# Third state of the streamed weight sum: added by VectorE from a tile already loaded, in place of an accumulating transfer

## The chip, the cores and the metric

The kernel runs on one core of one Trainium2 chip. The metric is the device time of one execution in microseconds; before the change it was 1002.07 us (median of 3 runs, 1001.94 to 1007.12). The engines are TensorE (PE, with PEld for its weight loads), VectorE (DVE), ScalarE (ACT), GpSimd (POOL) and SyncE (SP, which issues most transfers). POOL issues the transfers that add to what stands in SBUF.

## The reference

One layer of a residual block on 512 positions of width 1024, in float32: a gated feed-forward block, a mixer with two kinds of attention, a second gated feed-forward block, and a gated embedding at the end.

```python
def swiglu(x, w_gate, w_up, w_down):
    return (jax.nn.silu(x @ w_gate) * (x @ w_up)) @ w_down
...
f = swiglu(rms_norm(h, g_ffn1_pre[i]), w_ffn1_gate[i], w_ffn1_up[i], w_ffn1_down[i])
h = h + 0.5 * rms_norm(f, g_ffn1_post[i])
...
h = h + rms_norm(mixed @ w_out[i], g_mix_post[i])
f = swiglu(rms_norm(h, g_ffn2_pre[i]), w_ffn2_gate[i], w_ffn2_up[i], w_ffn2_down[i])
h = h + 0.5 * rms_norm(f, g_ffn2_post[i])
e = (p[i] @ w_ple_proj[i]) * jax.nn.sigmoid(h @ w_ple_gate[i])
h = h + rms_norm(e, g_ple_post[i])
```

The two feed-forward blocks have an inner width of 2816, 22 tiles of 128.

## The kernel before, in words

**Numbers as pairs.** Each float32 operand is split into a rounded part (hi) and the rest (lo), and a product is three matmuls: hi by hi, lo by hi, hi by lo (`mm3`, lines 247 to 250). The split of a weight chunk is made by ACT (wh, line 313) and DVE (wl = source minus wh, line 314).

**Seven products for eight.** Most of the feed-forward work is done in items: two column tiles of gate and up together (nine items per block, `(p,)`), or two by two tiles of the down matrix (four items per block, `(g, q)`, called down items here). An item is a 2x2 block product that is done with seven products instead of eight. Each of the seven, called op 0 to 6, multiplies a sum of input blocks (U0 to U6, or the v tiles) by a sum of weight blocks.

**Where the weight sums come from.** The four blocks of an item's weights, (0,0), (0,1), (1,0), (1,1), are added up in SBUF while they stream in. There are three kinds of tiles: x (three buffers), y (one buffer) and r. The table `SUMS` (line 164) says for each op which tile it reads, which block starts that tile, and which block is added to it after the op's split. A tile x goes through four states: (0,0) for op 0; plus (1,0) for op 2; plus (1,1) for op 3; plus (0,1) for op 5. A tile y has two: (1,1) for op 4; plus (1,0) for op 6. Op 1 reads a plain tile r. A start is a transfer on SP's queue (line 178), an addition an accumulating transfer on POOL's queue (`sum_in`, line 223), issued when the split that read the former state is done.

**The order.** `ORDER` (line 44) sets the ops of an item as 0, 1, 2, 4, 3, 6, 5, and items are interleaved: ops 3, 6, 5 of one item alternate with ops 1, 2, 4 of the next one. A chunk of weights is one op's tile; chunks are numbered in the order of use. `get` hands a chunk out, and `ensure` keeps the splits up to three chunks ahead (`LOOK`); split code is placed behind the evacuation of the op just issued (`behind("evac")`). PE's order is as written; the other engines' orders are made by a scheduler at build time, each engine then runs its instructions in order.

**Evacuations.** The products of an item share three PSUM banks, named f_a, f_b and f_c. DVE copies or adds them out: f_g (line 584), f_y (lines 588 and 597), f_x (line 591), and for down items f_f (line 629). They stand in DVE's order between the weight splits.

The lines that the change and the steps of the prediction touch: 164 (`SUMS`), 168 to 190 (`emit_dma`), 192 to 220 (`emit_split`), 222 and 223 (`sum_in`), 313 and 314 (split), 584 to 601 and 629 (evacuations).

Of the kernel before, what the change touches and what calls it, by code (L numbers as in the profile page):

```python
# [13 lines left out]
ALU = mybir.AluOpType  # L14
# [46 lines left out]
def block_kernel(ctx, tc, xT, pT, gains, ident_d, bias_d, wgu1, wst1, wd1, wdst1, wqk, wv, wo, wgu2, wst2, wd2, wdst2, wpp, wpg, gple, out):  # L61
    nc = tc.nc
    pe, act, dve, pool = nc.tensor, nc.scalar, nc.vector, nc.gpsimd
# [40 lines left out]
    chunks = []  # L104
# [39 lines left out]
    for kind, *at in PLAN:  # L144
        if kind == "qk":
            chunks.extend(qk_chunks[2 * at[0]:2 * at[0] + 2])
        else:
# [13 lines left out]
    pos, n_dma, n_split = [0], [0], [0]  # L161


    SUMS = {0: ("x", (0, 0), (1, 0)), 1: ("r", (0, 1), None), 2: ("x", None, (1, 1)), 3: ("x", None, (0, 1)),
            4: ("y", (1, 1), (1, 0)), 5: ("x", None, None), 6: ("y", None, None)}
    running = {}

    def emit_dma(cuts=1, queues=(nc.sync,)):
# [3 lines left out]
        if isinstance(n, tuple):  # L172
            op, item, n = n
            kind, block, _ = SUMS[op]
            if block is None:
# [16 lines left out]
    def emit_split(cuts=1, between=None):  # L192
        i = n_split[0]
        src, n = chunks[i]
        n_split[0] += 1
        add = None
        if isinstance(n, tuple):
            op, item, n = n
            kind, _, add = SUMS[op]
            r = raws.pop(i) if kind == "r" else running[kind, item]  # L200
        else:
            r = raws.pop(i)
        if i in apart:
            splits[i] = apart[i]()
            for q, (hi, lo) in enumerate(zip(*splits[i])):
                split_to(hi[:], lo[:], r[:, q * T:(q + 1) * T])
            return
        if i in late:
            hi, lo = late[i]()
        else:  # L210
            hi, lo = (wp.tile([P, 1024], F32R, name=f"w{q}{i}", tag=f"w{q}", bufs=4) for q in "hl")
        for q in range(cuts):
            a, b = q * n // cuts, (q + 1) * n // cuts
            with behind("evac"):
                marks["split"] = split_to(hi[:, a:b], lo[:, a:b], r[:, a:b])
            if between is not None and q == 0:
                between()
        splits[i] = (hi, lo)
        if add is not None:
            sum_in(r[:, :n], src[add[0], add[1]])  # L220

    def sum_in(r, block):
        pool.dma_start(out=r, in_=block, accum_op=ALU.add)  # L223
# [3 lines left out]
    def ensure(i):  # L227
        i = min(i, len(chunks) - 1)
        while n_split[0] <= i:
            while n_dma[0] < min(n_split[0] + (5 if n_dma[0] in deep else RAW), len(chunks)):  # L230
                emit_dma()
            emit_split()
# [78 lines left out]
    def split_to(hi, lo, src, g=None):  # L311
        if g is None:
            a = act.copy(hi, src)  # L313
            b = dve.tensor_tensor(lo, src, hi.bitcast(F32), ALU.subtract)  # L314
        else:
            a = act.activation(hi, src, AF.Copy, scale=g)
            b = dve.scalar_tensor_tensor(lo, src, g, hi.bitcast(F32), ALU.mult, ALU.subtract)
        return a.ins, b.ins

    @contextmanager  # L320
    def behind(*names):
        with ExitStack() as stack:
            for name in names:
                for ins in marks.get(name, ()):
                    stack.enter_context(tc.issue_after(ins))
            yield
# [419 lines left out]
    for j in range(4):  # L746
        if j == 0:
            nc.sync.dma_start(out=gt[:, :56], in_=gains)
        nc.sync.dma_start(out=h[:, 2 * j, :], in_=xT[2 * j * P:(2 * j + 1) * P, :])
        if j < RAW:  # L750
            emit_dma(1 if j else 2, (nc.sync,) if j else (nc.scalar, nc.sync))
        nc.sync.dma_start(out=h[:, 2 * j + 1, :], in_=xT[(2 * j + 1) * P:(2 * j + 2) * P, :])
        if j == 0:
            act.copy(tmp("table", 0)[:, 0:1], eps[:])
            emit_split(2, first_x)
            marks["first"] = marks.pop("evac") + marks["split"]
        for k in (2 * j, 2 * j + 1):
            if k:
                split_h(u, k, 0, T, G_F1PRE)
        if j:  # L760
            ensure(j)
        else:
            nc.sync.dma_start(out=ident[:], in_=ident_d)
# [19 lines left out]
    with tc.tile_pool(name="mx", bufs=1, reuse_waits="tile") as mp:  # L783
# [258 lines left out]
        for n in range(64 + LAG_AV):  # L1042
            if n < 64:
                s, r = divmod(n, 8)
# [211 lines left out]
```

## Time and profile before

| | |
|---|---|
| median of the runs | 1002.07 us (1002.07, 1001.94, 1007.12) |
| profiled execution, its own time | 1004.57 us |
| span of its trace | 1002.9 us |
| mean granted TensorE clock | 0.997 |
| moved by DMA | 139.71 MB, mean 139 GB/s |
| read from HBM | 134.31 MB |

A row of the profile gives a line, an engine, an operation and its tiles, then the busy time, the mean time of one, and the engine's idle time before it with what ended it. The chain of waits follows the work that ended last back through what released it. The span leaves out about 1.7 us of the execution around it. By stage: the first feed-forward block lies at about 20 to 335 us, the mixer at about 335 to 600 us, the second feed-forward block at about 600 to 925 us, the rest after that. How busy the engine queues and the DMA engines are over the span, in 40 equal slices of 25 us (tenths; GB/s moved):

```profile
DMA  7338887988886313313423311168879889975202
GB/s 284 101 103 189 165 173 189 196 184 187 193 190 174 118 35 115 95 54 98 123 83 98 89 60 53 53 147 173 189 171 206 192 171 204 194 186 190 61 3 85
```

The items fill the slices with 7 to 9 tenths.

### The profile page before, as it was taken

The page shows a single profiled execution, that of the slowest core. Times are in us where ns is not written, and L with a number is a line of the kernel's source. Part 1 is how long each engine was busy: PE and PEld are TensorE (multiplying, and loading weights), DVE is VectorE, ACT ScalarE, POOL GpSimd, SP SyncE. Part 2 cuts the span into 40 slices and gives each one's busy share as a digit, 9 for nine tenths or more (in the row PEclk, how much of TensorE's full clock was granted, in tenths as well). Part 3 has the DMA queues.
Part 4 walks back from the last instruction along what each step waited for, and adds up shares of the span by engine and source line. Part 5 has one row for each costly group of instructions (what it writes and reads, how often), then busy time and mean ns, then how long its engine had stood idle before and what let it go on. Part 6 is the DMA issues. An engine that isn't in the chain of part 4 may idle for free.

```text
span 1002.9 us, 18451 instructions
## 1 busy us (share of the span) xinstructions
PE 983.8 (98%) x7242; PEld 926.2 (92%) x7242; DVE 774.9 (77%) x1355; ACT 585.6 (58%) x977; POOL 134.6 (13%) x221
## 2 busy tenths in 40 slices
PE   9999999999999999999999999999999999999996
PEld 7889999999998999888898799889999999999886
DVE  6777777677666888999999868787687777676857
ACT  6456554464456366777789755465554664455563
POOL 0001112212120003344000000011122221210000
PEclk9999999999999999999999999999999999999998
DMA  7338887988886313313423311168879889975202
GB/s 284 101 103 189 165 173 189 196 184 187 193 190 174 118 35 115 95 54 98 123 83 98 89 60 53 53 147 173 189 171 206 192 171 204 194 186 190 61 3 85
DMA packets 44855, 139.71 MB, mean 139 GB/s; under 512 B 5216, under 2 KB 5600, under 8 KB 44768
## 3 DMA queue, kind: packets, MB, share of 16 engines
q0 software_dynamic: 14976, 50.34, 30.6%
q1 hardware_dynamic: 28368, 85.83, 25.2%
q10 hardware_dynamic: 1424, 2.36, 1.0%
q8 instruction: 57, 0.93, 0.4%
q14 instruction: 30, 0.25, 0.1%
HBM read 134.31 MB, written 2.10 MB: 136 GB/s over the span
## 4 chain that ended last, share of the span: by engine, by line
PE 70%; DMA 9%; issue 9%; DVE 7%; ACT 4%; POOL 0%; SPq 0%; POOLq 0%; DVEq 0%; ACTq 0%
PE f_a L248 6%; PE f_a L249 6%; PE f_a L250 6%; DMA wy<-in_wst_dram 3%; DMA wx<-in_wst_dram 3%; PE f_c L249 3%; PE f_c L248 3%; PE f_c L250 3%; PE pj L248 2%; DVE wl L314 2%; PE pj L250 2%; PE pj L249 2%; PE pt L929 2%; PE f_d L249 2%; PE f_d L250 2%
## 5 line engine op out<-in xcount | busy, mean ns | idle before, releaser
L314 DVE TENSOR_TENSOR wl<-wx,wh 128x1024 fp32r<-128x1024 f32 (+1 forms) x104 | 118.3, 1139 | 41.9 <-ACT wh L313 40.6
L313 ACT CAST wh<-wx 128x1024 fp32r<-128x1024 f32 (+1 forms) x104 | 101.7, 984 | 68.8 <-DMA wx<-in_wst_dram 39.2
L314 DVE TENSOR_TENSOR wl<-wr,wh 128x1024 fp32r<-128x1024 f32 (+2 forms) x100 | 109.2, 1098 | 27.3 <-ACT wh L313 26.6
L313 ACT CAST wh<-wr 128x1024 fp32r<-128x1024 f32 (+2 forms) x100 | 94.4, 951 | 44.3 <-DMA wr<-in_wgu_dram 13.8
L223 POOL DMA_DIRECT2D wx<-in_wst_dram x54 | 47.1, 872 | 405.3 <-DVE wl L314 356.4
L313 ACT CAST wh<-wy 128x1024 fp32r<-128x1024 f32 (+1 forms) x52 | 51.3, 986 | 52.7 <-DMA wy<-in_wdst_dram 24.3
L314 DVE TENSOR_TENSOR wl<-wy,wh 128x1024 fp32r<-128x1024 f32 (+1 forms) x52 | 59.2, 1138 | 20.3 <-ACT wh L313 20.3
L248 PE MATMUL pj<-um_hi,wh 128*128 128x512 f32 (+1 forms) x160 | 56.7, 354 | 1.2 <-DVE f_f L650 1.2
L249 PE MATMUL pj<-um_lo,wh 128*128 128x512 f32 (+1 forms) x160 | 55.6, 348 | 0.1
L250 PE MATMUL pj<-um_hi,wl 128*128 128x512 f32 (+1 forms) x160 | 55.7, 348 | 0.0
L248 PE MATMUL f_a<-f_U6h,wh 128*128 128x256 f32 x144 | 40.3, 280 | 0.7 <-DVE f_x L591 0.6
L248 PE MATMUL f_a<-f_U5h,wh 128*128 128x256 f32 x144 | 40.1, 279 | 0.3 <-DVE f_y L597 0.3
L248 PE MATMUL f_c<-f_U4h,wh 128*128 128x256 f32 x144 | 40.1, 279 | 0.0
L248 PE MATMUL f_a<-f_U0h,wh 128*128 128x256 f32 x144 | 40.1, 278 | 0.0
L249 PE MATMUL f_a<-f_U0l,wh 128*128 128x256 f32 x144 | 40.1, 278 | 0.0
L250 PE MATMUL f_a<-f_U0h,wl 128*128 128x256 f32 x144 | 40.1, 278 | 0.0
L248 PE MATMUL f_b<-f_U1h,wh 128*128 128x256 f32 x144 | 40.1, 278 | 0.0
L249 PE MATMUL f_b<-f_U1l,wh 128*128 128x256 f32 x144 | 40.1, 278 | 0.0
L250 PE MATMUL f_b<-f_U1h,wl 128*128 128x256 f32 x144 | 40.1, 278 | 0.0
L249 PE MATMUL f_c<-f_U4l,wh 128*128 128x256 f32 x144 | 40.1, 278 | 0.0
L250 PE MATMUL f_c<-f_U4h,wl 128*128 128x256 f32 x144 | 40.1, 278 | 0.0
L249 PE MATMUL f_a<-f_U5l,wh 128*128 128x256 f32 x144 | 40.1, 278 | 0.0
(453 smaller groups left out, 3852.7 us busy)
## 6 DMA issues: line engine op xcount, KB each, us to landing
wx<-in_wst_dram POOLq DMA_DIRECT2D x54, 512.0 KB, 5.7
wx<-in_wst_dram SPq DMA_DIRECT2D x18, 512.0 KB, 4.6
wy<-in_wst_dram SPq DMA_DIRECT2D x18, 512.0 KB, 5.8
wr<-in_wst_dram SPq DMA_DIRECT2D x18, 512.0 KB, 5.8
wy<-in_wst_dram POOLq DMA_DIRECT2D x18, 512.0 KB, 6.1
wx<-in_wdst_dram POOLq DMA_DIRECT2D x24, 384.0 KB, 5.9
wr<-in_wqk_dram SPq DMA_DIRECT2D x16, 512.0 KB, 3.9
wr<-in_wgu_dram SPq DMA_DIRECT2D x15, 512.0 KB, 4.3
```

Of the source, the lines that this page charges most:

```text
L223: pool.dma_start(out=r, in_=block, accum_op=ALU.add)
L248: pe.matmul(ps, hi, mh, start=start, stop=False, skip_group_check=skip)
L249: pe.matmul(ps, hi, ml, start=False, stop=False, skip_group_check=skip)
L250: pe.matmul(ps, lo, mh, start=False, stop=stop, skip_group_check=skip)
L313: a = act.copy(hi, src)
L314: b = dve.tensor_tensor(lo, src, hi.bitcast(F32), ALU.subtract)
L929: pe.transpose(pt[:, qi * P:(qi + 1) * P], aw[qi][:, (j - qi) * P:(j - qi + 1) * P], ident[:])
```

## The change

The x tile's third state, (0,0) + (1,0) + (1,1), is made by DVE. The accumulating transfer of block (1,1) after the split of op 2 is gone from the table. When the split of op 4 is emitted (op 4 comes between op 2 and op 3, and its tile y holds the plain block (1,1) at that time), DVE first adds y to x in place. The other two additions to x and the one to y stay transfers.

```diff
-    SUMS = {0: ("x", (0, 0), (1, 0)), 1: ("r", (0, 1), None), 2: ("x", None, (1, 1)), 3: ("x", None, (0, 1)),
+    SUMS = {0: ("x", (0, 0), (1, 0)), 1: ("r", (0, 1), None), 2: ("x", None, None), 3: ("x", None, (0, 1)),
             4: ("y", (1, 1), (1, 0)), 5: ("x", None, None), 6: ("y", None, None)}
...
             hi, lo = (wp.tile([P, 1024], F32R, name=f"w{q}{i}", tag=f"w{q}", bufs=4) for q in "hl")
+        if isinstance(chunks[i][1], tuple) and op == 4:
+            x = running["x", item]
+            with behind("evac"):
+                dve.tensor_tensor(x[:, :n], x[:, :n], r[:, :n], ALU.add)
         for q in range(cuts):
```

The order of PE and of SP's queue is the same before and after. Lines behind 211 move down by 4. In the rows below a tile's name carries its chunk (wx48 is the x tile of the item whose op 0 is chunk 48) and a running number after it.

On POOL, the transfers around the first block's second group of items stood like this before:

```order
L223 DMA wx41_1456<-in_wdst1_dram 128x768
L223 DMA wx48_1676<-in_wdst1_dram 128x768
L223 DMA wy54_1833<-in_wdst1_dram 128x768
L223 DMA wx55_1858<-in_wst1_dram 128x1024
L223 DMA wx48_1676<-in_wdst1_dram 128x768
L223 DMA wx55_1858<-in_wst1_dram 128x1024
L223 DMA wy61_2021<-in_wst1_dram 128x1024
```

The same place of POOL's order now:

```order
L227 DMA wx41_1455<-in_wdst1_dram 128x768
L227 DMA wy54_1832<-in_wdst1_dram 128x768
L227 DMA wx55_1857<-in_wst1_dram 128x1024
L227 DMA wx48_1675<-in_wdst1_dram 128x768
L227 DMA wy61_2020<-in_wst1_dram 128x1024
```

Of each x tile's three transfers the middle one is gone: wx48 ahead of wy54, and wx55 ahead of wy61. This is so for all 26 items.

On DVE, around the split of op 4 of the second down item (wl54; f_f is the evacuation of a down item's bank), the order was:

```order
L314 TENSOR_TENSOR wl52_1809<-wx48_1676,wh52_1808 128x768
L629 TENSOR_TENSOR f1_f_527<-f1_f_527,f1_b1_1_1813 128x2x256
L314 TENSOR_TENSOR wl53_1836<-wx41_1456,wh53_1835 128x768
L629 TENSOR_TENSOR f1_f_527<-f1_f_527,f1_a1_0_1567 128x2x256
L314 TENSOR_TENSOR wl54_1861<-wy54_1833,wh54_1860 128x768
L629 TENSOR_TENSOR f1_f_527<-f1_f_527,f1_c1_1_1865 128x2x256
L314 TENSOR_TENSOR wl55_1886<-wx55_1858,wh55_1885 128x1024
```

The same place of DVE's order now:

```order
L318 TENSOR_TENSOR wl52_1809<-wx48_1675,wh52_1808 128x768
L633 TENSOR_TENSOR f1_f_527<-f1_f_527,f1_b1_1_1812 128x2x256
L318 TENSOR_TENSOR wl53_1835<-wx41_1455,wh53_1834 128x768
L633 TENSOR_TENSOR f1_f_527<-f1_f_527,f1_a1_0_1567 128x2x256
L215 TENSOR_TENSOR wx48_1675<-wx48_1675,wy54_1832 128x768
L318 TENSOR_TENSOR wl54_1860<-wy54_1832,wh54_1859 128x768
L633 TENSOR_TENSOR f1_f_527<-f1_f_527,f1_c1_1_1865 128x2x256
L318 TENSOR_TENSOR wl55_1886<-wx55_1857,wh55_1885 128x1024
```

The addition (line 215) stands right ahead of the y tile's split wl54, and the evacuation of f_c and the next split follow that split as before. Apart from the additions, DVE's order and ACT's differ in one place at the start of each block's items, where the split of the second item's op 1 (wh22, wl22) has moved ahead of the splits of the input sums U6 and U5.

## The prediction, made before the run

> **What bounds the kernel now.** I read the page's first part, then the busy time by stage (the two feed-forward stages run from about 60 to 335 us and from about 650 to 925 us), then what TensorE waited for, since only TensorE's waits can be won back where it is busy throughout.
>
> ```profile
> PE 983.8 (98%) x7242; PEld 926.2 (92%) x7242; DVE 774.9 (77%) x1355; ACT 585.6 (58%) x977; POOL 134.6 (13%) x221
> ```
>
> ```profile
> 200.00:260.00 60.00, 59.39 (x521) 59.02 (x519) 45.13 (x58) 31.81 (x42) 11.31 (x13) 1.00 0.87 188
> 700.00:800.00 100.00, 99.65 (x864) 99.30 (x864) 76.31 (x95) 51.82 (x67) 18.69 (x22) 1.00 0.88 190
> ```
>
> The columns are the stretch, its length, busy time of PE, PEld, DVE, ACT and POOL, the granted clock, the DMA share, GB/s. TensorE is busy for 59.39 of 60 us and 99.65 of 100 us in stretches in which the change works; the DMA engines are next at 0.87 and 0.88, VectorE (DVE) third at about three quarters. So the kernel is held by TensorE there, with the transfers close behind.
>
> ```profile
> PE f_d L249 <- DVE f_sl L314: 0.9, 1, 0.9
> PE f_c L248 <- DVE f_f L629: 0.8, 1, 0.8
> PE f_a L248 <- DVE f_x L591: 0.6, 2, 0.3
> PE f_a L248 <- DVE f_f L629: 0.4, 1, 0.4
> PE f_a L248 <- DVE f_y L597: 0.3, 1, 0.3
> ```
>
> These are all waits of TensorE that lie in the feed-forward products (total us, times, longest): 0.9 + 0.8 + 0.6 + 0.4 + 0.3 = 3.0 us. No wait for a weight split (wh, wl) is among them. Whatever the change does well, it can win about 3 us here, unless the pace of the matmuls themselves changes.
>
> Who stands behind such a wait is seen at the largest one that concerns the y tile, in the timelines of ACT, DVE, PE and POOL (start, us, what, idle before it):
>
> ```profile
> 171.85 0.83 ACT L313 CAST wh<-wy 128x768 fp32r<-128x768 f32 x1 [2.90 <-DMA wy<-in_wdst_dram]
> 172.72 0.96 DVE L314 TENSOR_TENSOR wl<-wy,wh 128x768 fp32r<-128x768 f32 x1 [2.18 <-ACT wh L313]
> 173.59 0.68 DVE L629 TENSOR_TENSOR f_f<-f_f,f_c 128x512 f32<-128x512 f32 x1
> 174.42 0.36 PE L248 MATMUL f_c<-f_v,wh 128*128 128x256 f32 x1 [0.75 <-DVE f_f L629]
> 167.71 0.86 POOL L223 DMA_DIRECT2D wx<-in_wdst_dram  x1 [4.93 <-DVE wl L314]
> ```
>
> The y block landed late; ACT's rounding waited for it 2.90 us, DVE's split waited for ACT, the evacuation of the bank f_c stood behind that split in DVE's order, and TensorE waited 0.75 us for the bank. The transfer that was late ran beside an accumulating one that POOL had issued at 167.71: the one after op 2, which the change removes.
>
> **The change part by part.** Removed: one accumulating transfer per item. There are 26 items: nine pairs and four down items in each feed-forward block, so 18 of 512 KB and 8 of 384 KB.
>
> ```profile
> q0 software_dynamic: 14976, 50.34, 30.6%
> ```
>
> ```profile
> wx<-in_wst_dram POOLq DMA_DIRECT2D x54, 512.0 KB, 5.7
> wy<-in_wst_dram POOLq DMA_DIRECT2D x18, 512.0 KB, 6.1
> wx<-in_wdst_dram POOLq DMA_DIRECT2D x24, 384.0 KB, 5.9
> wy<-in_wdst_dram SPq DMA_DIRECT2D x8, 384.0 KB, 5.3
> ```
>
> 26 of the 104 accumulating transfers are a quarter of q0's bytes: (18 x 0.524 + 8 x 0.393) = 12.6 of 50.34 MB, so about a quarter of 30.6%, 7.6% of 1002.9 us = 77 us of all 16 engines. Spread over some 490 us of feed-forward products that takes the share of 0.87 down to about 0.71. POOL issues 26 x 0.86 us less, off any path. The other transfers should land earlier; I estimate about 1 us each, as the late y load of 384 KB above took 6.30 us (next fence) against a median of 5.3. The chain of waits has it there as the link that ended last (start, us, what):
>
> ```profile
> 165.45 6.30 DMA wy<-in_wdst_dram
> 171.81 2.21 issue
> 174.03 4.62 DMA wy<-in_wdst_dram
> ```
>
> Added: one DVE addition per item, both inputs and the output in SBUF. No such addition is in the trace, but a split of the same size is:
>
> ```profile
> L314 DVE TENSOR_TENSOR wl<-wy,wh 128x1024 fp32r<-128x1024 f32 x36 | 43.9, 1219 | 10.8 <-ACT wh L313 10.8
> L314 DVE TENSOR_TENSOR wl<-wy,wh 128x768 fp32r<-128x768 f32 x16 | 15.3, 954 | 9.5 <-ACT wh L313 9.5
> ```
>
> 18 x 1.22 + 8 x 0.95 = 29.6 us more of DVE. It stands right ahead of the y tile's split of op 4, and it needs that y block landed. Where DVE waits for the landing anyway, the addition runs while ACT makes wh (0.84 us for 128x768), and the split loses only 0.95 - 0.84, about 0.1 us. Where y landed long before, the split of op 4 and all behind it on DVE (the rest of DVE's order, the accumulation of y that POOL issues after this split) come 0.9 to 1.2 us later, until the next idle time of DVE. The 10.8 and 9.5 us idle ahead of the y splits alone and the 23.69 us of DVE idle in 700 to 800 us, against some six additions there (7 us), say that it is swallowed within an item. Bounds: nothing, or all 29.6 us if each addition held TensorE for its length. Since TensorE waits for no weight split in these stages now, I take the end near nothing: **+0.2 us**, all of it at the one place where the y chain feeds a plain product (f_sl, below).
>
> Moved: the third state of x is ready after the addition instead of after a transfer, one chunk before op 3 needs it; that path gets shorter. In ACT's order one weight cast passes two operand casts at the start of each feed-forward stage, and the two operands are used one and three chunks after that one; I cost it at nothing, and at 1.05 us twice if that cover is gone.
>
> Gone waits: the 0.8, 0.4, 0.3 and both 0.3 (0.6) follow a landing: behind the f_x and f_y waits stand rows such as
>
> ```profile
> 237.65 1.23 DVE L314 TENSOR_TENSOR f_v<-f_vw,f_v 128x1024 fp32r<-128x1024 f32 x1 [1.08 <-ACT f_v L313]
> 235.84 0.84 ACT L313 CAST wh<-wx 128x768 fp32r<-128x768 f32 x1 [0.40 <-DMA wx<-in_wdst_dram]
> 292.51 1.05 ACT L313 CAST wh<-wx 128x1024 fp32r<-128x1024 f32 x1 [1.87 <-DMA wx<-in_wst_dram]
> 303.69 1.05 ACT L313 CAST wh<-wy 128x1024 fp32r<-128x1024 f32 x1 [3.69 <-DMA wy<-in_wst_dram]
> ```
>
> and each is smaller than the 1 us I expect the landings to gain: -2.1 us. What is late next there is TensorE itself. The 0.9 us for f_sl I leave: it hangs on the last y accumulation (row at 303.69), which gains from the emptier queues and loses from the later split.
>
> The pace of the matmuls is the term that I can't settle:
>
> ```profile
> 82.00:145.00 63.00, 63.00 (x536) 62.96 (x535) 46.21 (x55) 36.19 (x49) 11.28 (x13) 1.00 0.84 176
> 192.00:234.00 42.00, 42.00 (x373) 42.00 (x372) 31.68 (x38) 23.81 (x34) 8.49 (x10) 1.00 0.89 184
> 676.00:727.00 51.00, 50.95 (x432) 50.73 (x432) 35.64 (x43) 28.75 (x38) 8.68 (x10) 1.00 0.84 182
> 784.00:826.00 42.00, 42.00 (x373) 42.00 (x372) 31.27 (x38) 25.06 (x35) 8.07 (x10) 1.00 0.90 185
> ```
>
> The same products run at 63.00/536 = 117.5 ns and 51/432 = 118 ns a matmul in two stretches, at 42/373 = 112.6 ns in two others, with no difference in clock or DMA share. The pace changes at waits and between products, so a wait that comes or goes can shift it. Bounds: all slow stretches turned fast, (536 + 432) x 4.9 ns = -4.7 us; the two fast ones turned slow, 746 x 4.9 ns = +3.7 us. I take 0.
>
> A rule of the Trainium skill speaks against giving DVE more work here. Two rows first:
>
> ```profile
> 177.41 1.22 DVE L314 TENSOR_TENSOR wl<-wr,wh 128x1024 fp32r<-128x1024 f32 x1
> 177.23 0.86 POOL L223 DMA_DIRECT2D wx<-in_wdst_dram  x1 [0.59 <-DVE wl L314]
> ```
>
> POOL's preparation of a transfer took 0.86 us beside a two-input DVE operation, and 0.86 us at 167.71 too. The Trainium skill's page "SBUF — State Buffer", section "SBUF: two separate sides", says that a transfer issued by GpSimd is starved of descriptors while DVE holds the port pair that both share; its section "Who interferes with whom" counts DVE instructions with two SBUF inputs among those that contend with GpSimd's reads. The trace doesn't agree for this pair of instructions: 0.86 us both times. By the rows I add nothing; what it would come to if it held is rival 5.
>
> **The sum.** -2.1 + 0.2 + 0 = -1.9 us. Against the profiled execution: span 1002.9 to 1001.0, its time 1004.57 to 1002.7. That execution stands 2.5 us above the median of the runs shown, 1002.07; the same difference from the median gives **1000.2 us**.
>
> **The rivals.**
> 1. Nothing moves: the landings gain, but the waits stay or are replaced by DVE's later evacuations, since DVE goes from about 76% to 82% in these stretches. 1002 us, between 1001.5 and 1003.5. For it: DVE runs without gap at 172.72 to 174.42. Against it: DVE is idle again within each item.
> 2. Slower, through the y chain. The single y buffer goes round: load, split of op 4, accumulation, split of op 6, next load. If the transfers don't land earlier, the addition lengthens this round by 0.95 us at the second down item of each of four groups, where the split (172.72 + 0.96) ended as TensorE ran dry: 4 x 0.95 = 3.8 us, and each such wait can put the following 125 matmuls on the slow pace, 4 x 0.6 = 2.4 us. Together +6.2: 1008.3 us. It decides as soon as DVE takes up the addition later than the landing. For it: no slack at 174.42. Against it: the competing transfer is the one that is removed.
> 3. The pace flips: a short wait early in both stages turns the slow stretches fast: -1.9 - 4.7 = -6.6, 995.5 us. For it: both paces occur at the same load. Against it: nothing in the change aims at it.
> 4. The change doesn't do what it says, because the addition is ordered where y lands too late and holds op 3: the order shows it right ahead of the op 4 split, so this is nearly excluded; it would cost 26 x 0.95 at most.
> 5. POOL's preparation of a transfer waits out a two-input DVE operation, so the 26 y accumulations, which now follow one more such operation, are issued up to 1.22 us later. TensorE would feel it at the four places of rival 2: 4 x 1.22 = 4.9, 1007.0 us. Against it: the two rows of 0.86 us. [...]
>
> **How the numbers follow.** Forecast (998 to 1001.5) 0.50, nothing moves 0.23, the y chain 0.12, the pace 0.11, rivals 4 and 5 0.02 each. About 0.5%, 5.0 us, is what a measurement here can tell from no change, so faster means below 997.1 and slower above 1007.1. Faster: the pace 0.11 and a tail of the forecast 0.02, 0.13. Slower: half of the y chain 0.06, rival 4 0.02, half of rival 5 0.01, 0.09. Same: 0.78. The range leaves out half of the pace case and most of the y chain: 996.5 to 1005.0.
>
> **What would show it.** Right: q0 at about 37.8 MB and 23%; DMA share about 0.71 in 200 to 260 and 700 to 800 us; 26 new DVE rows of 1.22 and 0.95 us; the five waits at 1 us or less in all; DVE at about 804 us. Wrong: new waits of TensorE on wl or wh, or on f_f at the down items (rival 2); equal waits with another number of matmuls in the same stretches (rival 3).

## The result, and the profile after

The change made the kernel slower by a little: 1007.19 us median (22 runs, 1003.64 to 1010.70) against 1004.53 us for before on the same chip, a ratio of 1.0034 with a 95% interval of 1.0024 to 1.0045 (the quotient of the two medians is 1.0027, inside it; one of before's 22 runs took 1981.92 us and isn't counted in the ratio). That is +3.4 us by the ratio where -1.9 us was forecast, and the time lies beyond the range's upper end, 1005.0. A part of that is the base: the median of before was 1002.07 us in the 3 runs shown and 1004.53 us in these 22. By the ratio alone the time would have been 1002.07 x 1.0034 = 1005.5 us, still outside. The profiled execution of the change took 1005.78 us (span 1004.1), 1.2 us more than that of before.

First the engines' busy time and the queue of the accumulating transfers, from the page of the changed kernel:

```profile
PE 985.5 (98%) x7242; PEld 927.6 (92%) x7242; DVE 801.6 (80%) x1381; ACT 585.3 (58%) x977; POOL 112.0 (11%) x195
...
q0 software_dynamic: 11232, 37.75, 22.2%
```

The same two stretches as before, by windows:

```profile
200.00:260.00 60.00, 58.50 (x511) 58.10 (x510) 47.61 (x60) 31.22 (x41) 7.84 (x9) 1.00 0.65 151
700.00:800.00 100.00, 99.55 (x856) 99.27 (x855) 80.54 (x98) 51.00 (x66) 13.04 (x15) 1.00 0.69 161
```

The change does what it says: 26 more VectorE instructions, q0 from 50.34 to 37.75 MB, the DMA share from 0.87 and 0.88 to 0.65 and 0.69. And TensorE does less in the same time: 511 matmuls instead of 521, 856 instead of 864. What TensorE waits for in the feed-forward products now:

```profile
PE f_a L252 <- DVE f_f L633: 1.8, 2, 1.3
PE f_d L253 <- DVE f_sl L318: 1.2, 2, 0.7
PE f_a L252 <- DVE f_x L595: 0.3, 2, 0.2
```

Of the five waits of 3.0 us three are gone (0.8, 0.6 and 0.3 us). The one of 0.4 us for f_f, near 260 us, has grown to 1.3 us at the same product. The one for f_sl, which is the split of an input of a product and no evacuation, now comes in both blocks, and three new ones for evacuations stand at other places; none is for a weight split in these stages, and the total is 3.3 us. One of the new ones, at 785.61 us, shows what the addition does to VectorE's order. VectorE's timeline ahead of it, where the down items of the second block's first group end and pairs begin (start, us, what, idle before it):

```profile
778.16 0.96 DVE L318 TENSOR_TENSOR wl<-wx,wh 128x768 fp32r<-128x768 f32 x1 [1.49 <-ACT wh L317]
779.04 0.68 DVE L633 TENSOR_TENSOR f_f<-f_f,f_a 128x512 f32<-128x512 f32 x1
779.64 1.22 DVE L215 TENSOR_TENSOR wx<-wx,wy 128x1024 f32<-128x1024 f32 x1
780.77 1.22 DVE L318 TENSOR_TENSOR wl<-wy,wh 128x1024 fp32r<-128x1024 f32 x1
781.91 1.22 DVE L318 TENSOR_TENSOR f_v<-f_vw,f_v 128x1024 fp32r<-128x1024 f32 x1
783.04 0.69 DVE L318 TENSOR_TENSOR f_v<-f_b,f_v 128x512 fp32r<-128x512 f32 x1
783.65 1.22 DVE L318 TENSOR_TENSOR wl<-wx,wh 128x1024 fp32r<-128x1024 f32 x1
784.78 0.68 DVE L633 TENSOR_TENSOR f_f<-f_f,f_a 128x512 f32<-128x512 f32 x1
```

And TensorE's:

```profile
784.77 0.28 PE L253 MATMUL f_c<-f_U4l,wh 128*128 128x256 f32 x1
784.89 0.28 PE L254 MATMUL f_c<-f_U4h,wl 128*128 128x256 f32 x1
785.61 0.36 PE L252 MATMUL f_a<-f_U0h,wh 128*128 128x256 f32 x1 [0.45 <-DVE f_f L633]
785.80 0.28 PE L253 MATMUL f_a<-f_U0l,wh 128*128 128x256 f32 x1
```

From 778.16 on VectorE has no gap. The addition (1.22 us) stands ahead of four splits, and the evacuation f_f behind them (784.78) ends too late for the bank f_a. In the kernel without additions (experiment 1) VectorE has 0.25 and 0.46 us of idle time between the same instructions, and TensorE doesn't wait here. The wait shows as 0.45 us, but from 784.89 to 785.61 it takes 0.72 us instead of 0.11, and the next start, at 785.80, comes 0.19 behind instead of 0.11. What follows is dearer still:

```profile
82.00:145.00 63.00, 62.84 (x536) 62.59 (x535) 49.66 (x57) 36.39 (x49) 8.68 (x10) 1.00 0.66 149
192.00:234.00 42.00, 41.82 (x369) 41.66 (x368) 33.33 (x42) 23.47 (x32) 6.88 (x8) 1.00 0.72 157
676.00:727.00 51.00, 51.00 (x436) 51.00 (x435) 40.14 (x47) 28.57 (x38) 6.69 (x8) 1.00 0.69 159
784.00:826.00 42.00, 41.55 (x354) 41.38 (x353) 32.90 (x39) 22.86 (x33) 6.08 (x7) 1.00 0.71 155
```

In 784 to 826 us, 354 matmuls stand where 373 stood before: 41.55 us / 354 = 117.4 ns each instead of 112.6, at a clock of 1.00. The stretch has fallen to the slow pace behind that wait: 354 x 4.8 ns = 1.7 us. So a wait that the view of waits prices at 0.45 us cost about 0.7 + 1.7 = 2.4 us. It need not go that way: in experiment 10 a wait of 0.49 us at the same place (785.52 us) left 346 matmuls in the 40 us from 786 on, in experiment 9 there were 342, as here, though no wait shows there. In the change the slow pace ended at 827 us with no wait, behind the matmuls of the next group's first down product: from 828 to 868 us there are 353 matmuls.

### The profile page after: what moved, and what is told of

Its sections match the earlier page's. It is cut to its first block, busy times and chain, and to the rows that moved or that the text cites. A ratio compares the mean times of both kernels' runs of the same rounds, so it can differ in the third digit from the quotient of the medians.

```text
span 1004.1 us, 18401 instructions
## 1 busy us (share of the span) xinstructions
PE 985.5 (98%) x7242; PEld 927.6 (92%) x7242; DVE 801.6 (80%) x1381; ACT 585.3 (58%) x977; POOL 112.0 (11%) x195
## 3 DMA queue, kind: packets, MB, share of 16 engines
q0 software_dynamic: 11232, 37.75, 22.2%
## 4 chain that ended last, share of the span: by engine, by line
PE 70%; DVE 9%; DMA 9%; issue 7%; ACT 4%; POOL 0%; SPq 0%; ACTq 0%; DVEq 0%; POOLq 0%
PE f_a L252 6%; PE f_a L253 6%; PE f_a L254 6%; DVE wl L318 3%; DMA wx<-in_wst_dram 3%; DMA wx<-in_wdst_dram 3%; PE f_c L252 3%; PE f_c L253 3%; PE f_c L254 3%; PE pj L252 2%; PE pj L254 2%; PE pj L253 2%; PE pt L933 2%; ACT wh L317 2%; PE f_d L253 2%
## 5 line engine op out<-in xcount | busy, mean ns | idle before, releaser
L318 DVE TENSOR_TENSOR wl<-wy,wh 128x1024 fp32r<-128x1024 f32 (+1 forms) x52 | 59.2, 1138 | 13.2 <-ACT wh L317 13.2
L227 POOL DMA_DIRECT2D wx<-in_wst_dram x36 | 31.4, 872 | 252.8 <-DVE wl L318 227.6
L227 POOL DMA_DIRECT2D wy<-in_wst_dram x18 | 15.7, 870 | 244.9 <-DVE wl L318 244.9
L253 PE MATMUL f_a<-f_U6l,wh 128*128 128x256 f32 x144 | 40.1, 279 | 0.0
```

The source lines that it names most:

```text
L253: pe.matmul(ps, hi, ml, start=False, stop=False, skip_group_check=skip)
```

## The experiments

Theory A: fewer transfers do bring the gain, and VectorE's additions take more than that, as they delay the evacuations behind them. Each experiment is compared with before on its own chip.

**1. Neither transfer nor addition.**

```diff
-        if isinstance(chunks[i][1], tuple) and op == 4:
-            x = running["x", item]
-            with behind("evac"):
-                dve.tensor_tensor(x[:, :n], x[:, :n], r[:, :n], ALU.add)
```

> The accumulating transfer after op 2 is left out and nothing takes its place, so block (1,1) is missing from the x sums of ops 3 and 5. Every engine's order is otherwise that of before. Theory A (the addition's time on VectorE delays what stands behind it, and the relief of the DMA engines is worth little): 0 to 2 us under before, ratio 0.998 to 1.000, q0 at 37.8 MB. Theory B (taking the transfers out shifts the landings of the others and with them the waits, the addition costs nothing): slower than before by the 3 us of the change, ratio about 1.003. Theory C (any shift of the timing throws the pace of the matmuls by some us, either way): anywhere from 0.996 to 1.004.

Measured: 0.9965 (0.9952 to 0.9978), 1000.04 us. The relief alone is worth 3.5 us, more than the 2.1 us of the forecast, and the additions cost 1.0034 - 0.9965 = 0.0069, 6.9 us. The 7242 matmuls are the same in the same order, so the two profiled executions can be compared matmul by matmul: the change's last one starts 6.1 us behind this kernel's, of which 3.6 us are lost in the items of the first block and 2.4 us in those of the second, 4.9 us in all by single starts more than 0.06 us late and 1.2 us by the pace. The only wait left in the items' stages is of a kind that the forecast left, too, but it lies in the second block now; the one that the forecast saw, in the first block, is gone (waits of TensorE in this kernel):

```profile
PE f_d L249 <- DVE f_sl L314: 0.9, 1, 0.9
```

**2. Both: all transfers kept, and an addition of the same size and place** (y + y into a tile that the split overwrites).

```diff
-                dve.tensor_tensor(x[:, :n], x[:, :n], r[:, :n], ALU.add)
+                dve.tensor_tensor(lo[:, :n], r[:, :n], r[:, :n], ALU.add)
```

with the table's entry for op 2 as before.

> All transfers are kept, and an addition of the same size (y plus y, written to the tile that the split of op 4 then overwrites) stands on VectorE at the place of the change. Theory A: slower than before by 3 us or more, since the addition's cost comes without relief: ratio 1.003 to 1.006. Theory B: like before, ratio 1.000. Theory C: anywhere from 0.996 to 1.004.

Measured: 1.0114 (1.0086 to 1.0141). Without the relief the additions cost 11.4 us: gain and cost aren't independent terms. These additions don't touch x, so the cost isn't that x's third state comes late. Among the waits (same view, this kernel) there is now a long one for a weight split on ACT:

```profile
PE f_a L251 <- ACT wh L316: 3.6, 1, 3.6
PE f_a L251 <- DVE f_x L594: 2.4, 4, 1.3
```

**3 and 4. The change in the 18 pairs only, and in the 8 down items only.** The same table entry as before, and

```diff
+            if op == 2 and len(item) == 1:
+                add = None
...
-        if isinstance(chunks[i][1], tuple) and op == 4:
+        if isinstance(chunks[i][1], tuple) and op == 4 and len(item) == 1:
```

for the pairs; `len(item) == 2` for the down items.

> The change in the 18 pairs alone; the 8 down items keep their transfers. Theory A: if the cost lies in the down items, where the weight chunks follow each other every 2 us and an evacuation stands behind the split, this is like before or a little faster (ratio 0.998 to 1.001); if it lies in the pairs, where 18 of the 26 additions are, it is 1.003. Theory B: 1.002. Theory C: no pattern.

> The change in the 8 down items alone; the 18 pairs keep their transfers. Theory A with the cost in the down items: ratio 1.003 and waits of TensorE for f_f evacuations; with the cost in the pairs: 1.000. Theory B: 1.001. Theory C: no pattern.

Measured: pairs 1.0043 (1.0027 to 1.0060), down items 0.9999 (0.9984 to 1.0014). The loss sits in the pairs; in the down items, where rival 2 put it, what 8 additions cost and what 8 transfers less gain cancel within 1.5 us. Why the pairs lose isn't shown by this: an addition is longer there (1.22 us), and there are more of them.

**5. The additions on GpSimd.**

```diff
-                dve.tensor_tensor(x[:, :n], x[:, :n], r[:, :n], ALU.add)
+                pool.tensor_tensor(x[:, :n], x[:, :n], r[:, :n], ALU.add)
```

> The change, but with all 26 additions made by GpSimd instead of by VectorE, at the same place of the program; the transfers are as in the change. Theory A (the relief of the transfers is worth about 3.5 us, and the addition costs about 7 us because it takes VectorE's time ahead of evacuations and splits that stand behind it): VectorE is as in the kernel with neither transfer nor addition (ratio 0.9965), so 0.996 to 0.999 of before, about 1001 us, VectorE near 772 us busy; waits of TensorE for f_x, f_y and f_f nearly gone. Rival C (the third state of x comes too late through the addition, whoever makes it, and op 3 waits): GpSimd is no faster than VectorE's 1.22 us, so 1.003 or more, with waits for the x splits. Rival D (the two engines hinder each other in SBUF): two-input operations of VectorE get longer than 1.22 us, or the GpSimd addition takes several us, and the ratio stays at 1.002 to 1.010.

Measured: 1.0221 (1.0193 to 1.0248), 1026.89 us: far slower, as rival D had it. VectorE's groups by line and shape, of this kernel:

```profile
L318 DVE TENSOR_TENSOR wl<-wx,wh 128x1024 fp32r<-128x1024 f32 x72 | 110.8, 1541 | 13.1 <-ACT wh L317 12.3
L318 DVE TENSOR_TENSOR wl<-wr,wh 128x1024 fp32r<-128x1024 f32 x72 | 87.5, 1220 | 21.2 <-ACT wh L317 21.1
L318 DVE TENSOR_TENSOR wl<-wy,wh 128x1024 fp32r<-128x1024 f32 x36 | 51.2, 1421 | 14.3 <-ACT wh L317 14.1
```

and the addition itself, from its line's view (shortest, median and longest in ns, first and last start):

```profile
L215 POOL TENSOR_TENSOR wx<-wx,wy x26: 1844/2407/3313, 74.0 to 903.2; 128x1024 f32<-128x1024 f32 x18, 128x768 f32<-128x768 f32 x8
```

An addition takes GpSimd 2.4 us (median over both sizes), and the splits beside it take VectorE 1541 and 1421 ns on average instead of 1219 to 1222. VectorE is busy for 811.0 us, more than with the additions on it (801.6). So this run tells nothing on what the change would cost with VectorE relieved. (The ratio is beyond rival D's 1.010; its mechanism is what the rows show.) The Trainium skill's page "SBUF — State Buffer", section "Who interferes with whom", says that a VectorE instruction with two inputs in SBUF contends with a GpSimd instruction that reads SBUF; these rows agree.

**6 and 7. Half of the addition, and a sliver of it.** Same place, same waits:

```diff
-                dve.tensor_tensor(x[:, :n], x[:, :n], r[:, :n], ALU.add)
+                dve.tensor_tensor(x[:, :n // 2], x[:, :n // 2], r[:, :n // 2], ALU.add)
```

and `[:, :32]` for the sliver.

> The change with the VectorE addition cut to the first half of the columns (512 or 384 of 1024 or 768); the other half of block (1,1) is missing from the x sums of ops 3 and 5. Theory A: the cost goes with the time that VectorE loses: about half of the 7 us, or less if small delays are swallowed, so 0.997 to 1.001 of before (about 1001 to 1004 us). Rival B (it is the place, VectorE waiting in order for the y block's landing, not the length): as the change, 1.002 to 1.005.

> The change with the VectorE addition cut to 32 columns; the rest of block (1,1) is missing from the x sums of ops 3 and 5. Order and waits are those of the change, the time on VectorE is about 0.1 us each. Theory A: as without any addition, 0.995 to 0.998 of before, about 1000 to 1001 us. Rival B (place and wait): 1.002 to 1.005, as the change.

Measured: half 0.9984 (0.9967 to 1.0001), sliver 0.9963 (0.9945 to 0.9981). The additions by line, of the sliver (shortest, median and longest in ns, first and last start), then of the half and of the change (busy us, mean ns | idle of VectorE before them):

```profile
L215 DVE TENSOR_TENSOR wx<-wx,wy x26: 179/182/185, 76.7 to 881.4; 128x32 f32<-128x32 f32 x26
```

```profile
L215 DVE TENSOR_TENSOR wx<-wx,wy 128x512 f32<-128x512 f32 (+1 forms) x26 | 16.7, 641 | 0.8 <-DMA wy<-in_wdst_dram 0.8
```

```profile
L215 DVE TENSOR_TENSOR wx<-wx,wy 128x1024 f32<-128x1024 f32 (+1 forms) x26 | 29.5, 1134 | 0.2 <-DMA wy<-in_wdst_dram 0.2
```

This is the run that decides. With 26 x 0.18 = 4.7 us of additions the kernel is as fast as with none; 29.5 us cost 6.9 us. The intervals of the sliver and of the change are far apart, so place and order are free and the length isn't. The half, 16.7 us, lies between, 1.9 us over experiment 1; its interval overlaps the sliver's, so that the first half is nearly free and the second isn't is suggested, not shown.

**8. The addition emitted behind the split of op 4.** The same four lines stood behind the split, without `behind("evac")`.

> The change with the addition emitted right behind the y tile's split of op 4 instead of ahead of it, ahead of the y accumulation. The split of op 4 no longer waits for the addition, the evacuation behind both still does, and the third state of x is ready a split later. Theory A, if the late evacuations are what costs: 1.002 to 1.005, as the change. Variant E (the late split of op 4, and with it the late round of the y tile, is what costs): 0.997 to 1.000.

Measured: 1.0162 (1.0137 to 1.0186). The edit didn't do what was meant: without that call the scheduler put the addition one to four places earlier in VectorE's order than in the change, still ahead of the split of op 4, and there it waits for the y block to land:

```profile
L220 DVE TENSOR_TENSOR wx<-wx,wy 128x1024 f32<-128x1024 f32 (+1 forms) x26 | 29.7, 1141 | 33.0 <-DMA wy<-in_wst_dram 25.3 <-DMA wy<-in_wdst_dram 7.6
```

VectorE stood idle 33.0 us ahead of the additions, with what stands behind them queued up. Variant E isn't tested by it. It does price an in-order engine's wait: with the change's own order that idle time is 0.2 us.

**9 and 10. All items but pairs 4 and 5, and these two alone** (`item not in ((4,), (5,))`, `item in ((4,), (5,))` in the conditions of 3).

> The change in all items but the pairs 4 and 5 of each block, whose third state comes by the transfer as before (22 additions, 4 of the old transfers). Theory A (the addition costs where evacuations behind it have least room; in the run with the addition cut to 32 columns the evacuation of the bank f_a before U0, 193 and 783 us, had 0.15 and 0.31 us left, f_x of pair 5 0.29 us, where most others had 0.9 us or more): the larger part of the 7 us lies at these two pairs, so 0.997 to 1.001 of before. Rival F (the cost is spread evenly over the pairs): 14 of 18 pairs keep theirs, so 1.001 to 1.004.

> The change in pairs 4 and 5 of each block alone (4 additions, 22 of the old transfers stay). Theory A: nearly the whole cost of the additions and a sixth of the relief, so 1.002 to 1.006 of before, with waits of TensorE for f_f ahead of U0 and for f_x of pair 5. Rival F: 4 of 18 of the cost, 1.5 us, less 0.5 us of relief, so 0.999 to 1.002.

Measured: 1.0010 (0.9983 to 1.0036) and 1.0017 (1.0000 to 1.0035). Both results lie where both theories allow them. That the cost is concentrated at these two pairs isn't shown.

**11. Two splits of v tiles behind the evacuation.**

```diff
-            split_to(e2[:, 0], e2[:, 1], b4[:, 0::2])
...
-            split_to(e4[:, 0], e4[:, 1], w)
-            split_to(e1[:, 0], e1[:, 1], b4[:, 3:4])
+            with behind("evac") if r == 0 else behind():
+                split_to(e2[:, 0], e2[:, 1], b4[:, 0::2])
+                split_to(e4[:, 0], e4[:, 1], w)
+                split_to(e1[:, 0], e1[:, 1], b4[:, 3:4])
```

> The change, with one thing moved: where a group of down items ends and pairs begin, the splits of the v tiles that VectorE had kept for then (1.22 and 0.69 us) stand behind the next evacuation of the bank f_a instead of ahead of it. VectorE's work is the same. Theory A (late evacuations behind the additions are the cost): the waits for f_f ahead of U0 near 193 and 785 us go, worth 0.5 to 2 us with the pace behind them, so 1.000 to 1.003 of before. Rival G (it is VectorE's total time, whichever work stands first): 1.003 to 1.006, with the same waits a chunk or two later.

Measured: 1.0034 (1.0013 to 1.0055), nothing gained. The waits ahead of U0 are gone, as theory A had it, and these have come (waits of TensorE, this kernel):

```profile
PE f_d L253 <- DVE f_sl L318: 1.9, 2, 1.0
PE f_a L252 <- DVE f_f L634: 1.4, 1, 1.4
...
PE f_a L252 <- ACT f_g L589: 0.7, 1, 0.7
```

So one crowded place can be cleared, and the time doesn't change. Rival G isn't borne out either: the same waits don't come a chunk or two later. The new ones lie elsewhere, and ahead of the largest (1.4 us at 855 us, and both for f_sl) ACT waited 3.5 to 4.3 us for a landing.

**Late landings.** They were the forecast's reason for the gain. Transfers by median time from issue to landing, of the changed kernel and then of experiment 1:

```profile
wx<-in_wst_dram POOLq DMA_DIRECT2D x36, 512.0 KB, 6.3
wx<-in_wst_dram SPq DMA_DIRECT2D x18, 512.0 KB, 3.6
...
wx<-in_wdst_dram POOLq DMA_DIRECT2D x16, 384.0 KB, 5.7
```

```profile
wx<-in_wst_dram POOLq DMA_DIRECT2D x36, 512.0 KB, 5.7
wx<-in_wst_dram SPq DMA_DIRECT2D x18, 512.0 KB, 3.6
...
wx<-in_wdst_dram POOLq DMA_DIRECT2D x16, 384.0 KB, 5.1
```

Before, these accumulations took 5.7 and 5.9 us, but over three per item, where two are left. The removed ones (in POOL's order, those ahead of each y accumulation) were the quick ones, 5.5 and 4.7 us in the median; the two that stay took 6.0 us for the pairs and 6.1 us for the down items. Without the additions the same transfers land 0.4 us (pairs) and 0.9 us (down items) sooner; with them 0.4 us sooner for the down items and 0.2 us later for the pairs.

With the change's largest wait (1.33 us, near 258 us) the windows and ACT's timeline show this:

```profile
248.00:252.00 4.00, 4.00 (x37) 4.00 (x37) 3.20 (x5) 0.91 (x2) 0.88 (x1) 1.00 1.00 162
252.00:255.00 3.00, 3.00 (x28) 3.00 (x28) 2.33 (x3) 0.77 (x1) 0.00 (x0) 1.00 0.97 337
255.00:258.00 3.00, 3.00 (x28) 2.94 (x26) 0.23 (x1) 0.83 (x1) 0.00 (x0) 1.00 0.06 21
```

```profile
256.90 0.83 ACT L317 CAST wh<-wx 128x768 fp32r<-128x768 f32 x1 [4.13 <-DMA wx<-in_wdst_dram]
```

From 255 us on the DMA engines are busy for 0.06 of their time, and ACT waits on until 256.80, when the transfer has landed: a small rest of it trails behind. In the run with the sliver the same transfer, in the same order, took 4.85 instead of 8.27 us. Instructions come over the same engines, 57 loads of 16 KB in the page's list of queues (before and after alike; by their number TensorE's, as 7242 matmuls and as many weight loads are 254 for each):

```profile
q8 instruction: 57, 0.93, 0.4%
```

and one such load, with another of 8 KB, fell into the flight of the very y block on which the forecast's timeline rests (165.45 to 171.75 us; the loads at 167.82 and 167.53). Hence runs 12 to 14 below.

**What stands behind the new waits.** Of the change's six waits in the items' stages only the one at 785.61 us has nothing but VectorE's own order ahead of it. Ahead of the other five, 2.9 of the 3.3 us, ACT waits for a landing, as it did before the change. Beside the row of 256.90 above, for example (ACT's timeline, ahead of an f_x wait and of an f_sl wait):

```profile
129.52 1.05 ACT L317 CAST wh<-wx 128x1024 fp32r<-128x1024 f32 x1 [1.88 <-DMA wx<-in_wst_dram]
301.75 1.05 ACT L317 CAST wh<-wy 128x1024 fp32r<-128x1024 f32 x1 [2.85 <-DMA wy<-in_wst_dram]
```

The additions have a hand in this, too. They stand ahead of the split of op 4, and POOL issues the y accumulation behind that split. Measured against the matmul that TensorE has reached, the y accumulations are issued 0.04 us later than in experiment 1 with the sliver, 0.56 us with the half and 0.95 us with the change (means of 26), and land as much later. The x accumulations are issued only 0.12 us later with the change, but land 0.66 us later; why wasn't tested. ACT's casts of y tiles then wait longer, the longer the addition is (experiment 1, half, change; busy us, mean ns | idle of ACT before them):

```profile
L313 ACT CAST wh<-wy 128x1024 fp32r<-128x1024 f32 (+1 forms) x52 | 51.4, 988 | 37.5 <-DMA wy<-in_wst_dram 14.6 <-DMA wy<-in_wdst_dram 14.4 <-PE f_a L250 3.9
L317 ACT CAST wh<-wy 128x1024 fp32r<-128x1024 f32 (+1 forms) x52 | 51.3, 987 | 46.0 <-DMA wy<-in_wdst_dram 23.3 <-DMA wy<-in_wst_dram 20.1 <-DVE wl L318 2.2
L317 ACT CAST wh<-wy 128x1024 fp32r<-128x1024 f32 (+1 forms) x52 | 51.3, 986 | 53.4 <-DMA wy<-in_wst_dram 26.9 <-DMA wy<-in_wdst_dram 23.1 <-PE f_a L254 1.5
```

So the length of the addition can reach TensorE by two paths: over the evacuations behind it in VectorE's order, as theory A has it, and over the later y accumulation and the landings, as variant E has it. How the 6.9 us divide between them stays open, since experiment 8, which was to separate them, changed the order otherwise; in the traces, single executions, most of the waits are on the second.

**12 to 14. The instruction loads shifted** by half of their spacing (change, before) and by a quarter (change), with dummy matmuls of one column at the start:

```diff
-WARM = 9
+WARM = 3
...
+    for _ in range(38):
+        pe.matmul(warm[:, :1], acc[:, :P], acc[:, :1], start=True, stop=True)
```

(22 for the quarter.)

> The change with 38 dummy matmuls of one column in place of 6 of the 9 warm-up matmuls at the start, so that TensorE's instruction stream is some 128 instructions longer ahead of the first product, half of the spacing of the 16 KB instruction loads. Theory A (the cost is the additions' time on VectorE): within 0.15% of the change, 1.002 to 1.005, a shift at the start left aside. Rival H (the cost hangs on which transfers an instruction load falls into): it moves by 0.2% or more in either direction, and the wait of 1.3 us for f_f near 258 us goes or turns up elsewhere.

> The kernel before with the same 38 dummy matmuls. Theory A: within 0.15% of before, 0.9985 to 1.0015. Rival H: a change of 0.2% or more, and other waits of TensorE in the feed-forward products than the five of 3.0 us.

> The change with 22 dummy matmuls, a shift by some 64 instructions, a quarter of the spacing. Theory A: 1.002 to 1.005, as the change and as the half shift. Rival H: another ratio than the half shift by 0.2% or more.

Measured: 1.0154 (1.0140 to 1.0168), 1.0135 (1.0122 to 1.0148), 1.0105 (1.0085 to 1.0125). The dummies cost far more at the start than thought: up to the first pair 14.5 us in both half shifts and 8.2 us in the quarter, so only the difference of kernels with the same start is clean. Half shifted, the change against before is 1.0154 / 1.0135 = 1.0019, 1.9 us, with about 0 to 3.8 us as its interval; unshifted it is 3.4 us. The waits of TensorE with the half shift, of the change and then of before:

```profile
PE f_a L252 <- DVE f_x L595: 1.0, 2, 0.6
PE f_d L253 <- DVE f_sl L318: 0.9, 1, 0.9
PE f_a L252 <- DVE f_f L633: 0.6, 2, 0.3
...
PE f_a L252 <- ACT wh L317: 0.3, 1, 0.3
```

```profile
PE f_a L248 <- DVE f_x L591: 2.4, 2, 1.9
```

Other waits in both, the wait of 1.33 us gone from the change. With the start taken off, before moved by -0.1% and the change by -0.25% (half) and -0.1% (quarter), each with an uncertainty of 0.13 to 0.22%: the first and the last as theory A, the middle one nearer to rival H, none far beyond the noise. Which waits there are depends on such a shift; how much of the time does isn't shown. Whether the instruction loads themselves make landings late stays open, as the dummies move the start of the transfers against the work, too.

No version here that does all the work beats before: experiments 1, 6 and 7 leave work out, and the down items alone equal before.

## Why the prediction was wrong, point by point

- **What bounds the kernel**: right. TensorE's 3.0 us of waits were about all there was to win; 3.5 us were won without the additions. (The list of waits leaves out three of 1.0 us in all for the plain products at 5 to 23 us, one of them for a weight split; no item lies there.)
- **Gone waits, -2.1 us**: the sign was right, and without the additions 3.5 us (2.2 to 4.8) were won, and all four waits that the step counted are gone there. With the change three of them are gone and the fourth, of 0.4 us, is 1.3 us long. The reason was half right: the 1 us sooner that each transfer was to land is seen for the start of x (4.6 to 3.6 us) and the down items' x accumulations (0.9 us), for the pairs' only 0.4 us, and the pairs' plain loads of y took 6.7 us instead of 5.8. With the additions much of it is lost again. The timeline that carried this step has another candidate beside the removed transfer, the instruction loads.
- **The addition, +0.2 us, "swallowed within an item"**: this step failed. It measured 6.9 us, inside its bounds of nothing to 29.6, far from the end that was taken. The argument saw that the rest of VectorE's order and the y accumulation come 0.9 to 1.2 us later, but ended the delay at VectorE's next idle time, which it counted over 100 us (23.69 us for 7 us of additions), and it asked only which weight split TensorE waits for. The runs show that the delay isn't swallowed: evacuations behind the addition have no room at some places (785.61 us), and the y accumulations are issued 0.95 us later in the mean. VectorE's idle time ahead of the y splits is itself time in which ACT waits for such landings, so a later accumulation makes it longer instead of using it up (10.6 us in experiment 1, 13.2 us with the change). In the stretch of 700 to 800 us VectorE's busy time rose by 4.2 us while TensorE fell 8 matmuls behind, of 0.11 us each. Half an addition cost 1.9 us, not clear of the noise.
- **Pace 0**: the forecast called it unsettled, and it stays so: the stretch at 784 us lost 1.7 us to the slow pace in the profiled execution.
- **Moved parts** (x's third state sooner, two casts): right as far as seen; no wait for an x split came, ACT waited 0.5 us in all for an addition, and VectorE 0.2 us for a y block.
- **GpSimd's preparation** (rival 5): the transfers' issue didn't slow down, 862 to 865 ns in the median of the runs with an addition on VectorE, 865 before. The forecast set this against a page, but read the page too widely: the section "Who interferes with whom" of the Trainium skill's page "SBUF — State Buffer" infers that a `tensor_tensor` doesn't hold up descriptors, and the medians agree. The contention with GpSimd's reads is there, but it took GpSimd arithmetic to bring it out (experiment 5).
- **The rivals**: the first named the mechanism, waits "replaced by DVE's later evacuations", and priced it at nothing. The second put the delay at the down items, where experiment 4 finds none in sum; its mechanism, a longer round of the y tile, is what the later y accumulations show. The third happened in small, in the wrong direction.

## What to carry to other kernels

Idle time of an in-order engine summed over a stretch doesn't say that new work fits: look at each instruction behind the new one on which the bound engine waits, at the transfers that are issued behind it, and at their room. Idle time that is spent waiting for a transfer is no room if the new work delays that transfer. Compare the landings of the same transfers, not the medians of rows whose members have changed; and a single late landing in a trace doesn't say what made it late. A wait of the bound engine can cost several times what the view of waits shows, so compare the number of its instructions in equal stretches as well.

## What the runs showed of the hardware

- A stop of TensorE costs more than its idle time: 0.45 us idle came with 0.61 us between starts beyond the usual 0.11, and 0.08 us at the next start. The pace behind it can stay at 117.4 instead of 112.6 ns a matmul for over 40 us at a full clock; in the change it ended behind a down product, with no wait. A wait doesn't always bring the slow pace (experiment 10), and what sets it wasn't found.
- An addition takes GpSimd about twice as long as VectorE (2.4 against 1.22 us in the median of the 26), and with the splits beside it slowed VectorE is busy for 811.0 us, more than the 801.6 us with the additions on it.
- A transfer can land 1.8 us after the DMA engines have all but fallen still (share 0.06 from 255 us on, landing at 256.80): 8.27 us in flight, where it took 4.85 us in the same order in another execution.
- A matmul of one column isn't cheap: 76 of them (38 in float32, two passes each) took 16.21 us, 0.21 us each, where full weight loads of 128x128 go ahead of them.
